# A row of reciprocal roots on GpSimd, and a scaling issued ahead of a one-column product

## The chip, the cores and the metric

The kernel runs on one core of a Trainium2 chip. A core has five engines with a queue of instructions each: TensorE (PE, matrix products into PSUM), VectorE (DVE), ScalarE (ACT), GpSimd (POOL) and SyncE (SP, which here only issues transfers). They meet through semaphores. The metric is the device time of one launch in microseconds.

## The reference

One encoder layer over 512 tokens of 1024 channels, and 256 memory tokens. What matters here is the branch of cross-attention into the memory, and the end:

```python
def rms_norm(x, g):
    xf = x.astype(F32)
    y = xf * lax.rsqrt(jnp.mean(xf * xf, axis=-1, keepdims=True) + EPS)
    return (y * g.astype(F32)).astype(x.dtype)
...
        y_ml = mlstm_branch(ml_q, ml_k, ml_v, ml_o, ml_gates, w_ml_conv[l], b_ml_conv[l],
                            b_ml_igate[l], b_ml_fgate[l], ml_norm_g[l])
...
        mem_k, mem_v = jnp.split(rms_norm(mem, mem_norm_g[l]) @ w_mem_kv[l], 2, axis=-1)
        y_xa = memory_cross_attention(xa_q, mem_k, mem_v)
...
        x = x + merged @ w_out[l]
        x = x + conv_glu_ffn(rms_norm(x, ffn_norm_g[l]), w_ffn_up[l], w_ffn_conv[l], b_ffn_conv[l], w_ffn_down[l])
    return rms_norm(x, final_norm_g)
```

The factor of `rms_norm` is one number a token. The kernel takes it out of the products and applies it to what they give.

## The kernel before, in words

Channels lie on the 128 partitions and tokens along the free axis until the last part. A weight block of 128 rows is loaded by SP (`emit_raw`), and split into a high part (`wh`, ScalarE, line 242) and the rest (`wl`, VectorE, line 243, from the two SBUF tiles `wr` and `wh`); each product is then three matmuls (`mm3`, lines 260 to 262). `weights(key)` keeps the split one block ahead of the matmuls: the split of block i+1 is issued when block i begins.

While the projections run, a generator for the bidirectional mLSTM (`ml_all`) is advanced by `step`. Each of its blocks `block(h, J)` makes a score tile on PE, a chain on VectorE (lines 800 to 814, among them line 805, a maximum over two small SBUF tiles, and line 810, which adds the two directions of the score tile `E`), then PE turns the tile (line 819) and multiplies it with the values (line 825). At a head's end a power of four columns runs on GpSimd (line 834).

The order on each engine is set when the kernel is built, from the program's order and the planner's own costs; `tc.issue_after(x)` ties instructions behind one that is given. At run time every engine takes its queue in order.

**The memory's norm.** During the projection "o" the squares of the memory are summed over channels by a matmul with ones (`square_sums`, line 355), so that every partition holds the row of sums of 256 tokens, in PSUM. Two things are made of it. `rstd_wide` (lines 369 to 377) makes the row of 1/rms on every partition: Ln and Exp(-0.5 x) on ScalarE, and three VectorE passes that improve the result by one Newton step. `rstd_cols` (lines 358 to 366) makes the same numbers as columns, one a partition: two VectorE reductions against the identity and a GpSimd power -0.5 of 128 x 2. The row `mrb` is first used at line 1165, where the first block of memory keys leaves PSUM; the columns `mrc` at line 1177, where the memory values do. Four PSUM banks (`mm`) hold the results of projections in turn.

**The end.** The last product is cut so that the last 128 tokens (row tile 3) end in two halves of their first 512 channels: one in `pa_[1]`, the other in `pl`. The second half's sum of squares is taken over 257 columns, the last being an extra column that carries the sum so far (line 1519, `rest`, written beside the matmuls' result in the bank `pl`). Row tile 2 (the second last 128 tokens) gets its factor `col2` by a GpSimd power (line 1360), its second half of channels is scaled on ScalarE (line 1518), its first half on VectorE (`scaled(2, 0, col2)`, line 1366), and one transfer stores it (line 1523). Row tile 3 ends with a power (line 1526), scalings (lines 1527 to 1530) and two transfers (lines 1528 and 1531).

Of the kernel before, what the change touches and what calls it, by code (L numbers as in the profile page):

```python
# [11 lines left out]
F32 = mybir.dt.float32  # L12
F32R = mybir.dt.float32r
AF = mybir.ActivationFunctionType
ALU = mybir.AluOpType
AX = mybir.AxisListType

P = 128
S = 512
D = 1024  # L20
KT = D // P
NT = S // P
M = 256
# [98 lines left out]
def hybrid_block(ctx, tc, xg, xT, memT, wflat, vecs, gbias, nabias, out):  # L122
    nc = tc.nc
    V, A, G, PE, SY = nc.vector, nc.scalar, nc.gpsimd, nc.tensor, nc.sync

    cp = ctx.enter_context(tc.tile_pool(name="cp", bufs=1))
# [10 lines left out]
    def nm(s):  # L137
        uid[0] += 1
        return f"{s}_{uid[0]}"

    def unit(dt=F32):
        return up.tile([P, UNIT], dt, tag="unit", name=nm("u"))

    def scr(n=512):
        return sp.tile([P, S], F32, tag="scr", name=nm("s"))[:, :n]

    def tiny(n):
        return tp.tile([P, 32], F32, tag="tiny", name=nm("y"), bufs=12)[:, :n]
# [174 lines left out]
    nhalf = cp.tile([P, 16], F32, name="nhalf")  # L323
    G.memset(nhalf, -0.5)
    msk = []
    for d in range(2):
        sgn = 1 if d == 0 else -1
        m = cp.tile([P, P], F32, name=f"msk{d}")
# [16 lines left out]
    def two_parts(acc, ntok):  # L345
        h, l = [sp.tile([P, S], F32R, tag="scr", name=nm("s"))[:, :ntok] for _ in range(2)]
        A.activation(h, acc, AF.Copy)
        V.tensor_tensor(l, acc, h.bitcast(F32), op=ALU.subtract)
        return h, l

    def square_sums(parts, ntok):

        ps = atps()
        for i in range(2):
            st["mm"] = PE.matmul(ps[:, :ntok], onesr, parts[i], start=i == 0, stop=i == 1).ins
        return ps

    def rstd_cols(ps, ntok, tag, n=D):

        nt = ntok // P  # L360
        v, junk = tiny(nt), scr(P)
        for t in range(nt):
            V.tensor_tensor_reduce(junk, ps[:, t * P:(t + 1) * P], ident, 1.0 / n, 0.0, ALU.mult, ALU.add,
                                   accum_out=v[:, t:t + 1])
        col = cp.tile([P, nt], F32, name=f"rc_{tag}")
        st["pool"] = G.tensor_tensor(col, v, nhalf[:, :nt], op=ALU.pow).ins
        return col

    def rstd_wide(ps, ntok, tag, n=D):

        v, y = scr(ntok), scr(ntok)
        rb = cp.tile([P, ntok], F32, name=f"rb_{tag}", tag=f"rb{ntok}", bufs=1)
        A.activation(v, ps[:, :ntok], AF.Ln, scale=1.0 / n)
        A.activation(y, v, AF.Exp, scale=-0.5)
        V.scalar_tensor_tensor(v, ps[:, :ntok], -0.5 / n, y, op0=ALU.mult, op1=ALU.mult)
        V.tensor_tensor(v, v, y, op=ALU.mult)
        V.scalar_tensor_tensor(rb, v, 1.5, y, op0=ALU.add, op1=ALU.mult)
        return rb
# [76 lines left out]
    def proj(key, XHs, XLs, n=S, at={}, ps=None):  # L455

        ws = weights(key)
        if (key[0], key[1]) in SUMS or key[0] in SUMS:
            sum_step(SUMS.get(key[0]) or SUMS[key[:2]], ws)
        k0 = 0 if ps is None else 1  # L460
        if ps is None:
            ps = mmps()
        for k in range(k0, KT):
            mm3(ps[:, :n], ws[k][0], ws[k][1], XHs[k], XLs[k], k == 0, k == KT - 1)
            if k == 1:
                flush()
            if k in at:
                at[k]()
        return ps
# [655 lines left out]
    def step(n=1):  # L1125
        quota[0] += n
        while quota[0] >= 1 and gens:
            try:
                next(gens[0])
                quota[0] -= 1  # L1130
            except StopIteration:
                gens.pop(0)
        if not gens:
            quota[0] = 0.0
# [11 lines left out]
    for f in range(4):  # L1146
        ps = proj(("o", f), XH, XL, at={3: lambda: step(RB / 2)})
        t = scr()
        V.tensor_tensor(t, ps, rb, op=ALU.mult)
        if f == 0:  # L1150
            so.append(unit())
        A.activation(so[0][:, f * S:(f + 1) * S], t, AF.Tanh, scale=0.5)
        if f == 0:
            msum = two_parts(macc, M)
        if f == 1:

            with tc.issue_after(st["mm"]):
                mps = square_sums(msum, M)
            mrb, mrc = rstd_wide(mps, M, "m"), rstd_cols(mps, M, "m")
        step(RB / 2)  # L1160
    mkv = unit()
    mk, mv = mkv[:, 0:1024], mkv[:, 1024:2048]
# [17 lines left out]
    for f in range(4):  # L1180
        ps = proj(("naq", f), XH, XL, at={3: lambda: step(RB / 2)})
        V.tensor_tensor(nq[:, f * S:(f + 1) * S].rearrange("p (b r c) -> p b r c", r=ROWS, b=4), rv(ps), rv(rb),
                        op=ALU.mult)
# [103 lines left out]
    def cv(t, f):  # L1287
        o = t % 2 * D + f * S
        return C[t // 2][:, o:o + S]
# [49 lines left out]
    ss = [sv[:, 2 * t:2 * t + 2] for t in range(NT)]  # L1339
# [16 lines left out]
    def power(t, v, f):  # L1356

        col = tiny(1)
        V.tensor_tensor(col, ss[t][:, f:f + 1], v, op=ALU.add)
        G.tensor_tensor(col, col, nhalf[:, :1], op=ALU.pow)  # L1360
        return col

    def scaled(t, f, col, dst=None):

        dst = cv(t, f) if dst is None else dst
        V.scalar_tensor_tensor(dst, cv(t, f), col, gfin[:, f * S:(f + 1) * S], op0=ALU.mult, op1=ALU.mult)
# [122 lines left out]
    vs = {}  # L1489
# [21 lines left out]
    col2 = power(2, vs[2], 0)  # L1511
    sqa = squares(pa_[1][:, one_], 3, 0)
    v = tiny(1)
    V.tensor_tensor(v, ss[3][:, 0:1], vs[3], op=ALU.add)
    col = tiny(1)
    G.tensor_tensor(col, v, nhalf[:, :1], op=ALU.pow)
    with tc.issue_after(sqa):
        A.activation(cv(2, 1), cv(2, 1), AF.Copy, scale=col2)
    rest = V.scalar_tensor_tensor(pl[:, Hf:Hf + 1], v, D ** 0.5, col, op0=ALU.mult, op1=ALU.mult).ins
    with tc.issue_after(rest):  # L1520
        V.tensor_tensor(oa[:, one_], pa_[1][:, one_], gfin[:, one_], op=ALU.mult)
        scaled(2, 0, col2)
    SY.dma_start(out[2 * P:3 * P, :], C[1][:, :D])
    v, sq, col = tiny(1), scr(), tiny(1)
    A.activation(sq[:, :Hf + 1], pl[:, :Hf + 1], AF.Square, scale=D ** -0.5, accum_out=v)
# [114 lines left out]
```

## Time and profile before

| | us |
|---|---|
| median of 3 runs | 858.49 (857.82 to 859.49) |
| profiled execution | 858.62 |
| its span | 856.9 |
| PE busy | 849.4 (99%) |
| VectorE busy | 644.7 (75%) |
| ScalarE busy | 482.0 (56%) |
| GpSimd busy | 164.2 (19%) |

A row of the timeline gives the start, the duration, the engine, the line of the kernel, the operation, the tile written and the tiles read, their shapes and a count; in brackets stands how long the engine was idle before it and what ended that. "PEclk" is the granted clock of TensorE, 1.00 at its full speed. In the view of windows the columns are the window, its length, then busy time and count for PE, the loads of PE, VectorE, ScalarE and GpSimd, then the clock, the busy share of the 16 DMA engines and GB/s.

### The profile page before, as it was taken

To read this page: it belongs to the slowest core of one execution; us is meant where nothing else is said; L and a number is where in the kernel's file an instruction comes from. 1 tells how busy PE (TensorE), PEld (TensorE's weight loads), DVE (VectorE), ACT (ScalarE), POOL (GpSimd) and SP (SyncE) were. 2 spreads that over 40 slices of the span, in tenths; PEclk is the share of its full clock that TensorE was granted. 3 is DMA by queue.
4 is the path that set the end of the run, shared out by engine and by line. 5 is a ranking of instruction groups with operands and counts; after the bars stand their busy time and mean duration, and the time that the engine had idled before them with its cause. 6 is when DMAs were issued, how large, how long until landed. Compare 5 with 4: busy or idle time off the path is not lost.

```text
span 856.9 us, 12273 instructions
## 1 busy us (share of the span) xinstructions
PE 849.4 (99%) x4116; PEld 716.2 (84%) x4116; DVE 644.7 (75%) x1372; ACT 482.0 (56%) x1025; POOL 164.2 (19%) x279
## 2 busy tenths in 40 slices
PE   9999999999999999999999999999999999999996
PEld 7898988988888888888888888888888888888885
DVE  7696597877568758898668657877786777788886
ACT  7354456666546648888644445444464444446763
POOL 0100100001113594601101002222100333320001
PEclk9999999999999999999999999999999999999999
DMA  8226764643675655549755954677265222326663
GB/s 280 93 75 162 241 187 123 184 116 109 232 195 132 205 149 145 163 146 236 276 160 145 264 157 135 161 157 250 85 187 181 76 97 99 99 74 216 190 205 139
DMA packets 77023, 139.80 MB, mean 163 GB/s; under 512 B 38232, under 2 KB 45400, under 8 KB 75360
## 3 DMA queue, kind: packets, MB, share of 16 engines
q1 hardware_dynamic: 67184, 109.24, 40.6%
q0 software_dynamic: 9344, 29.39, 14.5%
q8 instruction: 32, 0.52, 0.2%
q10 hardware_dynamic: 432, 0.39, 0.1%
q14 instruction: 31, 0.25, 0.1%
HBM read 130.84 MB, written 31.21 MB: 189 GB/s over the span
## 4 chain that ended last, share of the span: by engine, by line
PE 97%; DVE 1%; DMA 0%; ACT 0%; issue 0%; POOL 0%; POOLq 0%; DVEq 0%
PE mm L260 25%; PE mm L262 25%; PE mm L261 25%; PE at L1330 2%; PE at L1328 2%; PE at L1329 2%; PE at L261 2%; PE at L260 2%; PE at L262 2%; PE mm L1330 1%; PE mm L1328 1%; PE mm L1329 1%; PE at L999 1%; PE at L980 1%; PE at L768 1%; PE at L792 1%
## 5 line engine op out<-in xcount | busy, mean ns | idle before, releaser
L260 PE MATMUL mm<-u,wh 128*128 128x512 f32 (+1 forms) x907 | 353.9, 390 | 0.0
L262 PE MATMUL mm<-u,wl 128*128 128x512 f32 (+1 forms) x907 | 350.2, 386 | 0.0
L261 PE MATMUL mm<-u,wh 128*128 128x512 f32 (+1 forms) x907 | 350.0, 386 | 0.0
L242 ACT ACTIVATE wh<-wr 128x512 fp32r<-128x512 f32 (+2 forms) x328 | 203.2, 625 | 172.6 <-PE mm L261 111.6
L243 DVE TENSOR_TENSOR wl<-wr,wh 128x512 fp32r<-128x512 f32 (+2 forms) x330 | 236.2, 719 | 62.7 <-ACT wh L242 56.6
L262 PEld LDWEIGHTS mm<-u,wl 128*128 128x128 f32 x907 | 170.5, 188 | 34.6
L260 PEld LDWEIGHTS mm<-u,wh 128*128 128x128 f32 x907 | 170.8, 188 | 33.1 <-ACT u L266 0.3
L261 PEld LDWEIGHTS mm<-u,wh 128*128 128x128 f32 x907 | 170.7, 188 | 33.1 <-DVE u L267 0.2
L618 POOL DMA_DIRECT2D u<-nav_d x128 | 62.7, 533 | 27.1 <-PE at L999 16.7
L1432 POOL TENSOR_TENSOR s<-s,rb 128x512 f32<-128x512 f32 x18 | 29.4, 1634 | 155.9 <-DVE s L1431 148.6
L169 POOL COPY y<-wl 128x1 f32<-128x1 f32 x24 | 5.9, 246 | 178.7 <-DVE wl L243 177.6
L1328 PE MATMUL at<-wh,u 128*128 128x512 f32 x100 | 39.1, 391 | 0.0
L1330 PE MATMUL at<-wh,u 128*128 128x512 f32 x100 | 38.9, 389 | 0.0
L1329 PE MATMUL at<-wl,u 128*128 128x512 f32 x100 | 38.9, 389 | 0.0
L1377 ACT ACTIVATE u<-r 128x256 fp32r<-128x256 f32 x44 | 17.7, 414 | 36.3 <-DVE r L1446 23.1
L518 ACT ACTIVATE s<-pad,vec 128x512 f32<-128x512 f32 x30 | 24.3, 811 | 19.1 <-DVE pad L516 19.1
L519 DVE SCALAR_TENSOR_TENSOR s<-pad,vec,s 128x512 f32<-128x512 f32 x30 | 23.0, 765 | 5.0 <-ACT s L518 4.9
L1428 ACT ACTIVATE s<-s 128x512 f32<-128x512 f32 x22 | 13.9, 633 | 19.9 <-DVE s L520 19.8
L1378 DVE TENSOR_TENSOR u<-r,u 128x256 fp32r<-128x256 f32 x44 | 20.4, 474 | 5.7 <-ACT u L1377 5.7
L1431 DVE SCALAR_TENSOR_TENSOR s<-s,s 128x512 f32<-128x512 f32 x22 | 15.2, 691 | 11.9 <-ACT s L1430 11.9
L520 DVE SCALAR_TENSOR_TENSOR s<-pad,vec,s 128x512 f32<-128x512 f32 x30 | 22.5, 748 | 0.7
L1330 PEld LDWEIGHTS at<-wh,u 128*128 128x128 f32 x100 | 18.8, 188 | 3.9
(343 smaller groups left out, 1249.4 us busy)
## 6 DMA issues: line engine op xcount, KB each, us to landing
wr<-wflat SPq DMA_DIRECT2D x140, 512.0 KB, 3.7
wr<-wsum_T SPq DMA_DIRECT2D x20, 512.0 KB, 4.1
wsum_T<-wflat POOLq DMA_DIRECT2D x8, 1024.0 KB, 9.0
wsum_T<-wflat POOLq DMA_DIRECT2D x6, 768.0 KB, 7.3
nab<-nabias SPq DMA_DIRECT2D x16, 256.0 KB, 2.8
u<-nav_d POOLq DMA_DIRECT2D x128, 32.0 KB, 2.9
s<-xT SPq DMA_DIRECT2D x15, 256.0 KB, 4.7
nav_d<-nv POOLq DMA_DIRECT2D x8, 256.0 KB, 2.9
```

The costliest lines, as they stand in the source:

```text
L242: st["hi"] = A.activation(h[:, u:v], src, AF.Copy).ins
L243: st["lo"] = V.tensor_tensor(l[:, u:v], src, h[:, u:v].bitcast(F32), op=ALU.subtract).ins
L260: PE.matmul(ps, lh, rh, start=start, stop=False)
L261: PE.matmul(ps, lh, rl, start=False, stop=False)
L262: st["mm"] = PE.matmul(ps, ll, rh, start=False, stop=stop).ins
L518: A.activation(t1, pad[:, 0:512], AF.Identity, scale=vcol(w, i), bias=vcol(b, i))
L519: V.scalar_tensor_tensor(t1, pad[:, 1:513], vcol(w, n + i), t1, op0=ALU.mult, op1=ALU.add)
L618: G.dma_start(vw[r * 32:(r + 1) * 32, i * 256:(i + 1) * 256], nav_v[hf, r, CW[b]:CW[b] + 32, hp * 256:(hp + 1) * 256])
L1328: PE.matmul(bank, ah[:, ts], w[0], start=start, stop=False, skip_group_check=True)
L1329: PE.matmul(bank, ah[:, ts], w[1], start=False, stop=False, skip_group_check=True)
L1330: st["mm"] = PE.matmul(bank, al[:, ts], w[0], start=False, stop=True, skip_group_check=True).ins
L1432: ve.tensor_tensor(c, c, rb2, op=ALU.mult)
```

## The change

Two places change. The row of the memory's 1/rms is no longer made by `rstd_wide`: ScalarE copies the sums out of PSUM, scaled by 1/1024, into `mv2`, the columns are made as before, and GpSimd raises the 256 columns of `mv2` to the power -0.5 (the exponent is the first column of `nhalf`, repeated). At the end, the scaling of row tile 2's first half is tied behind the sum `vadd` and stands ahead of the extra column in the program, where it was tied behind that column.

```diff
-            mrb, mrc = rstd_wide(mps, M, "m"), rstd_cols(mps, M, "m")
+            mrb, mv2 = cp.tile([P, M], F32, name="rb_m"), scr(M)
+            A.activation(mv2, mps[:, :M], AF.Copy, scale=1.0 / D)
+            mrc = rstd_cols(mps, M, "m")
+            G.tensor_tensor(mrb, mv2, nhalf[:, :1].to_broadcast([P, M]), op=ALU.pow)
...
-    V.tensor_tensor(v, ss[3][:, 0:1], vs[3], op=ALU.add)
+    vadd = V.tensor_tensor(v, ss[3][:, 0:1], vs[3], op=ALU.add).ins
     col = tiny(1)
     G.tensor_tensor(col, v, nhalf[:, :1], op=ALU.pow)
     with tc.issue_after(sqa):
         A.activation(cv(2, 1), cv(2, 1), AF.Copy, scale=col2)
+    with tc.issue_after(vadd):
+        scaled(2, 0, col2)
     rest = V.scalar_tensor_tensor(pl[:, Hf:Hf + 1], v, D ** 0.5, col, op0=ALU.mult, op1=ALU.mult).ins
     with tc.issue_after(rest):
         V.tensor_tensor(oa[:, one_], pa_[1][:, one_], gfin[:, one_], op=ALU.mult)
-        scaled(2, 0, col2)
```

## The prediction

> **What bounds the kernel now.** I read the page's engine row and chain of waits first, then who TensorE waits for, then the two places of the change by the timeline.
>
> ```profile
> PE 849.4 (99%) x4116; PEld 716.2 (84%) x4116; DVE 644.7 (75%) x1372; ACT 482.0 (56%) x1025; POOL 164.2 (19%) x279
> PE 97%; DVE 1%; DMA 0%; ACT 0%; issue 0%; POOL 0%; POOLq 0%; DVEq 0%
> PE at L289 <- PEq L1633: 0.8, 1, 0.8
> ```
>
> The third line is the whole answer of the view of waits for PE: in the whole span it waits once, 0.8 us at the start. So TensorE's stream sets the end, and the matmuls leave only the last microseconds to others. Work taken off another engine in the middle is worth nothing; a new wait of PE costs its full length, since no idle time is left to give it back. The profiled execution took 858.62 us, its span 856.9, so 1.7 lie around it; the median is 858.49, 0.13 less. Sums below start from 858.6.
>
> **The memory's row: what goes.**
>
> ```profile
> 130.50 0.41 PE L355 MATMUL at<-s,onesr 128*128 128x256 f32 x2
> 131.17 1.28 ACT L373 ACT_TABLE_LOAD   x1
> 132.47 0.38 ACT L373 ACTIVATE s<-at 128x256 f32<-128x256 f32 x1
> 132.87 1.28 ACT L1152 ACT_TABLE_LOAD   x1
> 134.70 0.40 ACT L374 ACTIVATE s<-s 128x256 f32<-128x256 f32 x1
> 131.31 0.68 DVE L243 TENSOR_TENSOR wl<-wr,wh 128x512 fp32r<-128x512 f32 x1
> 135.13 0.42 DVE L375 SCALAR_TENSOR_TENSOR s<-at,s 128x256 f32<-128x256 f32 x1 [3.14 <-ACT s L374]
> 136.23 0.42 DVE L377 SCALAR_TENSOR_TENSOR rb_m<-s,s 128x256 f32<-128x256 f32 x1
> 136.23 0.08 DVE L363 DVE_READ_ACCUMULATOR2_ANT y<- 128x1 f32 x1
> 136.40 0.84 POOL L366 TENSOR_TENSOR rc_m<-y,nhalf 128x2 f32<-128x2 f32 x1 [22.24 <-DVE y L363]
> 147.58 0.42 DVE L1165 TENSOR_TENSOR u<-mm,rb_m 128x256 f32<-128x256 f32 x1
> ```
>
> Gone are Ln and Exp (0.38 + 0.40), the load of Ln's table and of the one that brings the others back (2 x 1.28), and three VectorE passes, of which the first and last are shown (3 x 0.42). A Copy of Ln's shape (0.38) comes in. ACT gains 2.96 us, VectorE 1.26 and a wait of 3.14: all of it beside matmuls that never waited, so **0 on the path**.
>
> **What comes: one power over 256 columns.** No row has this shape. Bounds come from the power on few columns and from GpSimd's ordinary product on this shape:
>
> ```profile
> 849.40 0.55 POOL L1516 TENSOR_TENSOR y<-y,nhalf 128x1 f32<-128x1 f32 x1
> 230.68 1.04 POOL L834 TENSOR_TENSOR y<-y,nhalf 128x4 f32<-128x4 f32 x1 [7.21 <-DVE y L832]
> 232.21 0.69 DVE L1210 TENSOR_TENSOR s<-mm,rb_x 128x512 f32<-128x512 f32 x1 [1.68 <-PE mm L262]
> 184.59 1.25 POOL L834 TENSOR_TENSOR y<-y,nhalf 128x4 f32<-128x4 f32 x1 [23.53 <-DVE y L832]
> L1453 POOL TENSOR_TENSOR r<-r,u 128x256 f32<-128x256 f32 x9 | 6.6, 738 | 7.2 <-DVE u L1446 7.2
> ```
>
> One column 0.55, four 1.04, the latter with VectorE idle beside it (its 1.68 before 232.21): (1.04 - 0.55) / 3 = 0.163 us a column. 256 columns: 0.55 + 255 x 0.163 = **42.1 us**. The product's rate (0.74) is the lower end; the slowest four columns give (1.25 - 0.55) / 3 = 0.233 and 60 us. From two columns (0.84) to four it is 0.10, so 0.84 + 254 x 0.10 = 26 us. I take 42: same operation, measured undisturbed; the product does not compute a power. The doubt is that a long run may go by a faster loop than four columns.
>
> The Trainium skill, "GPSIMD Engine Reference", section 3.1, puts a two-input pass at about 2.6 cycles an element and core, at 1.2 GHz: an estimate from it is 0.55 us and a start-up for 256 columns, and the sum would be that of the rival "short power" below. The four columns speak against applying it to a power.
>
> When it starts: the sums are ready at about 131 and VectorE is free at 132.0. Its two column reductions lie between L375 and the last reading at 136.23, with one pass of 0.42 among them, so some 0.85 us; the small power took 0.84. That makes about 133.7 in the program's order. The row is there at 133.7 + 42.1 = **175.8**, where 136.65 was. The 11 us left until L1165 at 147.58 are used up, and 28 more.
>
> **Who waits: the shared input.** Two pairs show what an operation on GpSimd does to one on VectorE that reads two SBUF tiles:
>
> ```profile
> 556.79 0.73 POOL L1449 TENSOR_TENSOR r<-r 128x256 f32<-128x256 f32 x1 [1.71 <-DVE u L1378]
> 556.81 1.27 DVE L243 TENSOR_TENSOR wl<-wr,wh 128x512 fp32r<-128x512 f32 x1
> 31.25 1.03 POOL L366 TENSOR_TENSOR rc_x<-y,nhalf 128x4 f32<-128x4 f32 x1 [28.71 <-DVE y L363]
> 31.61 0.69 DVE L243 TENSOR_TENSOR wl<-wr,wh 128x512 fp32r<-128x512 f32 x1 [0.46 <-ACT wh L242]
> ```
>
> L243 takes 0.69 alone; beside a product of 256 columns it takes 1.27 and ends 0.56 after it: it did nothing until GpSimd had finished. Beside a power of four columns it takes 0.69: once four columns are read, nothing is held. With 256 columns reading lasts as long as computing, unless GpSimd can buffer most of them. So I expect VectorE's operations with two SBUF inputs to stand still from 133.7 to about 175.8. The Trainium skill, "SBUF — State Buffer", section "Who interferes with whom", has it that such a pair excludes each other for the whole instruction, whoever starts first; the second pair shows less than that for a short power, the first pair agrees.
>
> What is behind it on VectorE and PE:
>
> ```profile
> 137.71 0.16 DVE L805 SCALAR_TENSOR_TENSOR y<-y,em 128x2 f32<-128x2 f32 x1
> 139.79 0.35 DVE L810 SCALAR_TENSOR_TENSOR E<-E,y 128x128 f32<-128x128 f32 x1
> 140.33 0.27 PE L819 MATMUL at<-ident,E 128*128 128x128 f32 x1
> 148.24 0.68 DVE L243 TENSOR_TENSOR wl<-wr,wh 128x512 fp32r<-128x512 f32 x1
> 151.75 0.28 PE L262 MATMUL mm<-u,wl 128*128 128x256 f32 x1
> 850.00:850.50 0.50, 0.16 (x2) 0.00 (x0) 0.23 (x2) 0.21 (x2) 0.00 (x0) 1.00 0.00 0
> 853.50:854.00 0.50, 0.00 (x0) 0.00 (x0) 0.00 (x0) 0.00 (x0) 0.00 (x0) 0.50 0.96 365
> ```
>
> L805 reads two small SBUF tiles and begins the chain to L810, whose block PE turns at 140.33; PE is in order, so everything behind that turn waits. That chain took 2.4 us with other work between (137.71 to 140.14), and its two shown ends alone make 0.5. By the first, PE resumes at 175.8 + 2.4 = 178.2: **37.9 us lost**, 36.0 by the second. PE's clock falls from 1.00 to 0.50 some 3 us after its last matmul (the window rows at 850 and 853.5; the clock is the column ahead of the DMA share). After such a stall it starts slow; no row shows the way back. If it takes 3 us too, half of them are lost: an estimate of +1.5, bounds 0 and 3.
>
> If the power runs long but VectorE isn't shut out, L1165 alone waits, and behind it VectorE's queue: the split at 148.24 for the third memory block, whose matmuls follow about 151.8. VectorE comes to that split's end 1.3 us after L1165's start (148.92 - 147.58), so at 177.1, and PE loses 25.3.
>
> On GpSimd's own queue the heads' powers come next (184.59 is the second's), themselves behind VectorE; its transfers for weight sums are issued from the projection "nak" on, later in the program. They move with the rest.
>
> **The tail.**
>
> ```profile
> 849.47 0.72 ACT L1518 ACTIVATE u<-u,y 128x512 f32<-128x512 f32 x1 [0.49 <-POOL y L1360]
> 850.27 0.17 DVE L1519 SCALAR_TENSOR_TENSOR at<-y,y 128x1 f32<-128x1 f32 x1 [1.11 <-PE at L1330]
> 850.68 0.74 DVE L1366 SCALAR_TENSOR_TENSOR u<-u,y,u 128x512 f32<-128x512 f32 x1
> 851.03 0.81 POOL L1526 TENSOR_TENSOR y<-y,nhalf 128x1 f32<-128x1 f32 x1 [1.07 <-ACT s L1525]
> 851.50 0.33 SPq L1523 DMA_DIRECT2D out<-u  x1
> 852.64 0.33 SPq L1531 DMA_DIRECT2D out<-s  x1
> 852.00:852.50 0.50, 0.00 (x0) 0.00 (x0) 0.50 (x2) 0.50 (x1) 0.00 (x0) 1.00 0.38 147
> 852.50:853.00 0.50, 0.00 (x0) 0.00 (x0) 0.11 (x1) 0.09 (x1) 0.00 (x0) 1.00 1.05 426
> 854.50:855.00 0.50, 0.00 (x0) 0.00 (x0) 0.00 (x0) 0.00 (x0) 0.00 (x0) 0.50 1.00 365
> ```
>
> The scaling (L1366, 0.74) moves into VectorE's wait of 1.11 ahead of the extra column (L1519): its factor is there at 849.47, as ACT's use shows, so it ends at 850.21, and L1519, which waits for PE's last matmul, starts at 850.27 as before. Beside the last power it is gone: 0.81 falls towards 0.55, -0.26 on the path. The third tokens' transfer leaves at about 850.3, not 851.5. Today it and the last two share full engines from 852.5 to 855.0 (five half-microsecond rows, first and last shown under the row before them); 0.8 us lie from issue to first bytes (851.5 to 852.3, as that row's share of 0.38 has it). Moved, the last 512 KB start at 852.38 + 0.8 and take 1.3 at 400 GB/s: 854.5, where 855.05 was. **-0.55**, bounds -1.2 (the whole advance) and +0.5 (the scaling shuts out the power of L1516 that starts 0.07 before it).
>
> Sum: 858.6 + 37.9 + 1.5 - 0.55 = **897.5**.
>
> **The rivals.**
> - *Long power, VectorE not shut out* (0.20). For it: the pair at 31.25. 858.6 + 25.3 + 1.5 - 0.55 = 884.9.
> - *Middling power, 26 us* (0.11), by the step from two columns to four; against it, the two were measured beside VectorE. All is 15.9 us sooner: 881.6 shut out, 869 not.
> - *Short power* (0.29), the other side: the loop over many columns runs at up to 16 ns a column, near the product's 0.74 us in all. The row must then be there before L805 runs at 137.7, so a power of at most 4.0 us, or 13.9 (147.58 - 133.7) without shutting out. PE never waits, only the tail counts: 858.6 - 0.55 = 858.05, no change. For it: the same engine does 256 ordinary products in 0.74; against it: 0.163 a column.
> - *Faster* (0.03): the short power with the tail's whole advance and a little of PE's order: 856.7.
>
> **How the numbers follow.** The forecast has 0.37, at 897.5, its own range 892 (small power second in GpSimd's queue, no slow clock, quickest chain) to 900 (slow clock at its 3 us and the tail's +0.5). A measurement of this kernel can tell about 0.2%, 1.7 us, from no change. Slower: 0.37 + 0.20 + 0.11 = 0.68, and 0.02 of the short power at 10 us, shut out: 0.70. Same 0.27, faster 0.03. Without the short power 3 in 10 are left out, so the range goes down to it: 857.0 to 900. The 60 us power (915) stays outside.
>
> **What would show it.** Right: a POOL power at L1162 of about 42 us from 133 on, L243 or L805 stretched over it, PE idle from 140 to 178, PEclk at 0.5 in that slice. VectorE waiting at L1165 for POOL, with L243 at 0.69 before: the second case. A power of a few microseconds and no wait of PE: the short one, and my rate per column was wrong. Tail: L1366 ahead of L1519, the last power at 0.55, the third transfer's issue near 850.3, each counted from PE's end.

## The result, and the profile after

| | before | after |
|---|---|---|
| median, us | 858.5 (857.82 to 859.54) | 891.7 (890.69 to 891.82) |
| ratio | | 1.0382 [1.0368, 1.0395] |
| span of the profiled execution, us | 856.9 | 890.0 |

The change costs 33.2 us. The engine row and the chain of waits of the page after:

```profile
PE 853.0 (96%) x4116; PEld 719.5 (81%) x4116; DVE 644.6 (72%) x1369; ACT 479.5 (54%) x1022; POOL 205.5 (23%) x280
PE 92%; POOL 5%; DVE 1%; ACT 1%; DMA 0%; issue 0%; POOLq 0%; DVEq 0%; ACTq 0%
```

The whole list of what PE waited for after (total, times, longest):

```profile
PE at L825 <- ACT E L820: 28.4, 1, 28.4
PE at L768 <- ACT H L812: 1.3, 1, 1.3
PE at L289 <- PEq L1637: 0.8, 1, 0.8
```

GpSimd has come into the chain with 5% of the span, and PE, which had one wait of 0.8 us, has one of 28.4. Where from, the timeline after shows on GpSimd, VectorE, ScalarE and PE:

```profile
131.51 41.51 POOL L1162 TENSOR_TENSOR rb_m<-s,nhalf 128x256 f32<-128x256 f32 x1 [17.35 <-ACT s L1160]
173.01 0.69 POOL L366 TENSOR_TENSOR rc_m<-y,nhalf 128x2 f32<-128x2 f32 x1
132.99 0.16 DVE L805 SCALAR_TENSOR_TENSOR y<-y,em 128x2 f32<-128x2 f32 x1
134.02 0.35 DVE L810 SCALAR_TENSOR_TENSOR E<-E,y 128x128 f32<-128x128 f32 x1 [0.28 <-ACT E L809]
134.88 0.69 DVE L243 TENSOR_TENSOR wl<-wr,wh 128x512 fp32r<-128x512 f32 x1
173.73 0.16 DVE L808 TENSOR_TENSOR y<-y,ex 128x2 f32<-128x2 f32 x1 [33.48 <-POOL rc_m L366]
179.15 0.42 DVE L1168 TENSOR_TENSOR u<-mm,rb_m 128x256 f32<-128x256 f32 x1
173.99 0.37 ACT L812 ACTIVATE H<-at,y 128x128 f32<-128x128 f32 x1 [33.30 <-DVE y L808]
175.58 0.26 ACT L820 ACTIVATE E<-at 128x128 f32<-128x128 f32 x1
147.17 0.28 PE L262 MATMUL mm<-u,wl 128*128 128x256 f32 x1
175.90 0.80 PE L825 MATMUL at<-u,E 128*128 128x128 f32 x2 [28.45 <-ACT E L820]
180.83 0.56 PE L260 MATMUL mm<-u,wh 128*128 128x256 f32 x1
188.11 0.39 PE L825 MATMUL at<-u,E 128*128 128x128 f32 x2
```

Three things are to be seen. The power takes 41.51 us. While it runs, VectorE's operations with two SBUF inputs keep their length of before (L243 0.69 us, L805 0.16, L810 0.35): VectorE is not shut out. And VectorE doesn't wait where the row is used (L1168, line 1165 of before), but well ahead of it in its queue, at line 808, a tiny product that reads nothing GpSimd writes. The row names `rc_m` as what it waited for: the small power, which the planner put *behind* the long one.

Line 808 writes a fresh tile of the ring of tiny tiles, which has 12 buffers. In the built order its tile is the twelfth taken after the one that holds the memory's two column sums, which `rc_m` reads. In the program as built the two tiles have the same address. So the reading is: a buffer that can't be written until `rc_m` has read it.

From line 808 the wait reaches PE by way of ScalarE. Line 812 there needs what line 808 gives and stood for 33.30 us; line 820, which copies the turned tile out of PSUM for PE's line 825, comes behind it in ScalarE's queue, so PE stands too.

The loss by PE's place, each row against its counterpart before (before, the block of memory keys that starts here at 180.83 started at 148.91):

```profile
147.29 0.39 PE L825 MATMUL at<-u,E 128*128 128x128 f32 x2
148.91 0.36 PE L260 MATMUL mm<-u,wh 128*128 128x256 f32 x1
154.75 0.39 PE L825 MATMUL at<-u,E 128*128 128x128 f32 x2
```

L825 is 28.6 us late (175.90 against 147.29), the next block 31.9, the L825 after two blocks 33.4. The end of the span is 33.1 late, so the tail gave 0.3 back. The clock is in the windows of after (the number ahead of the DMA share):

```profile
145.00:150.00 5.00, 2.45 (x21) 2.24 (x19) 0.00 (x0) 0.00 (x0) 5.00 (x1) 1.00 0.00 0
150.00:155.00 5.00, 0.00 (x0) 0.00 (x0) 0.00 (x0) 0.00 (x0) 5.00 (x1) 0.50 0.00 0
183.00:184.00 1.00, 1.00 (x7) 1.00 (x7) 0.00 (x0) 0.43 (x1) 0.00 (x0) 0.50 0.04 12
184.00:185.00 1.00, 1.00 (x10) 1.00 (x10) 0.69 (x1) 0.20 (x1) 0.00 (x0) 0.94 0.00 0
```

It fell to half after PE's stop and came back at about 184.1. The two blocks from 180.83 took 7.28 us in place of 5.84: 1.4 us of half clock.

The tail after:

```profile
883.12 0.75 DVE L1369 SCALAR_TENSOR_TENSOR u<-u,y,u 128x512 f32<-128x512 f32 x1 [0.30 <-POOL y L1363]
883.29 0.28 PE L1333 MATMUL at<-u,u 128*128 128x256 f32 x1
883.79 0.16 DVE L1524 SCALAR_TENSOR_TENSOR at<-y,y 128x1 f32<-128x1 f32 x1
883.95 0.33 SPq L1527 DMA_DIRECT2D out<-u  x1
884.54 0.55 POOL L1530 TENSOR_TENSOR y<-y,nhalf 128x1 f32<-128x1 f32 x1 [0.93 <-ACT s L1529]
885.90 0.33 SPq L1535 DMA_DIRECT2D out<-s  x1
```

Counted from the end of PE's last matmul (883.57; 850.16 before): the scaling runs under the last matmuls, the third store leaves after 0.38 us (1.34 before), the last power takes 0.55 (0.81). The extra column starts at 0.22 (0.11), because the scaling ends late. The last store leaves at 2.33 (2.48).

### The profile page after: what moved, and what is told of

It reads as the page before. It is cut to its first block, busy times and chain, and to the rows that moved or that the text cites. A ratio compares the mean times of both kernels' runs of the same rounds, so it can differ in the third digit from the quotient of the medians.

```text
span 890.0 us, 12274 instructions
## 1 busy us (share of the span) xinstructions
PE 853.0 (96%) x4116; PEld 719.5 (81%) x4116; DVE 644.6 (72%) x1369; ACT 479.5 (54%) x1022; POOL 205.5 (23%) x280
## 4 chain that ended last, share of the span: by engine, by line
PE 92%; POOL 5%; DVE 1%; ACT 1%; DMA 0%; issue 0%; POOLq 0%; DVEq 0%; ACTq 0%
PE mm L260 24%; PE mm L261 24%; PE mm L262 24%; POOL rb_m L1162 5%; PE at L1331 2%; PE at L1333 2%; PE at L1332 2%; PE at L261 2%; PE at L260 2%; PE at L262 2%; PE mm L1331 1%; PE mm L1333 1%; PE mm L1332 1%; PE at L999 1%; PE at L980 1%; PE at L768 1%
## 5 line engine op out<-in xcount | busy, mean ns | idle before, releaser
L243 DVE TENSOR_TENSOR wl<-wr,wh 128x512 fp32r<-128x512 f32 (+2 forms) x330 | 236.3, 719 | 63.7 <-ACT wh L242 57.9
L1162 POOL TENSOR_TENSOR rb_m<-s,nhalf 128x256 f32<-128x256 f32 x1 | 41.5, 41508 | 17.4 <-ACT s L1160 17.4
L825 PE MATMUL at<-u,E 128*128 128x128 f32 x32 | 6.5, 286 | 28.4 <-ACT E L820 28.4
L825 PEld LDWEIGHTS at<-u,E 128*128 128x128 f32 x32 | 6.0, 196 | 29.7 <-ACT E L820 28.7
L808 DVE TENSOR_TENSOR y<-y,ex 128x1 f32<-128x1 f32 (+1 forms) x16 | 2.5, 156 | 33.8 <-POOL rc_m L366 33.5
L519 DVE SCALAR_TENSOR_TENSOR s<-pad,vec,s 128x512 f32<-128x512 f32 x30 | 23.0, 765 | 5.0 <-ACT s L518 4.9
```

What stands on the lines that cost most here:

```text
L243: st["lo"] = V.tensor_tensor(l[:, u:v], src, h[:, u:v].bitcast(F32), op=ALU.subtract).ins
L1162: G.tensor_tensor(mrb, mv2, nhalf[:, :1].to_broadcast([P, M]), op=ALU.pow)
```

## The experiments

All kernels but one were timed against the kernel of before; medians and ratios with their intervals.

**The buffer.** e1 gives the two column sums a buffer of their own:

```diff
-        v, junk = tiny(nt), scr(P)
+        v = tiny(nt) if tag != "m" else cp.tile([P, nt], F32, name="v_m")
+        junk = scr(P)
```

> The changed kernel, with a buffer of its own for the two column sums that the small power rc_m reads (before: one of the 12 buffers of the ring of tiny tiles). Theory A: the long wait of VectorE at L808 is for that ring buffer, which rc_m, queued behind the 41.5 us power, releases late. Then L808 no longer waits; VectorE goes on to the first use of the row (near 147) and waits there until the row is ready at 173.0. PE then has the second memory block's weights too and stops at about 152 instead of 147.45, resuming near 174.3: a stall of 22.3 us, with 3.6 us of slow clock and -0.3 at the end 858.5 + 25.6 = 884. Theory B: VectorE is shut out of the second SBUF input while the power runs, or waits for the row itself: VectorE stops at 140.3 as before and the time stays at 891.7.

Measured: 880.9 us, ratio 1.026 [1.0245, 1.0275]. Its timeline (lines are one higher here, so line 808 is L809):

```profile
139.53 0.16 DVE L809 TENSOR_TENSOR y<-y,ex 128x2 f32<-128x2 f32 x1
172.29 0.42 DVE L1169 TENSOR_TENSOR u<-mm,rb_m 128x256 f32<-128x256 f32 x1 [25.43 <-POOL rb_m L1163]
173.57 0.58 PE L262 MATMUL mm<-u,wl 128*128 128x256 f32 x1 [20.52 <-DVE wl L243]
```

The wait at line 808 is gone and a new one of 25.4 us has come at the row's first use; PE stands 20.5 us in the third memory block, for its weights' low part. Theory A's mechanism holds, B falls. The time is 3 us below A's number: PE ran to 153.0, not 152, was let go at 173.6, not 174.3, and by the windows its clock was back 4.3 us after the first matmul, where the changed kernel took 8.2.

**The order on GpSimd.** e2 ties the long power behind the small one:

```diff
+            with tc.issue_after(st["pool"]):
-            G.tensor_tensor(mrb, mv2, nhalf[:, :1].to_broadcast([P, M]), op=ALU.pow)
+                G.tensor_tensor(mrb, mv2, nhalf[:, :1].to_broadcast([P, M]), op=ALU.pow)
```

> The changed kernel, with the power over the row tied behind the small power rc_m on GpSimd's queue. Theory A (ring buffer): rc_m ends near 133.4 and frees its buffer, L808 doesn't wait; the row is ready at about 174.9, 1.9 us later than with its own buffer, and its first use waits: stall 24.2 us, about 886. Theory B (shut out): VectorE stops at its first operation with two SBUF inputs near 133.4, and the time is 891 to 895.

Measured: 882.81 us, ratio 1.0283 [1.0266, 1.0301].

```profile
132.79 0.73 POOL L366 TENSOR_TENSOR rc_m<-y,nhalf 128x2 f32<-128x2 f32 x1 [18.62 <-DVE y L363]
133.51 41.12 POOL L1163 TENSOR_TENSOR rb_m<-s,nhalf 128x256 f32<-128x256 f32 x1
140.55 0.16 DVE L808 TENSOR_TENSOR y<-y,ex 128x2 f32<-128x2 f32 x1
174.66 0.42 DVE L1169 TENSOR_TENSOR u<-mm,rb_m 128x256 f32<-128x256 f32 x1 [27.02 <-POOL rb_m L1163]
```

The ring is untouched here, and line 808 runs at 140.55 without a wait: it was the small power's place in the queue that held its buffer. Again A holds and B falls; the time is 3 us below A's 886, since PE waited 22.1 us and not 24.2. This is also the order that the prediction assumed, so it shows what that order costs: 24.5 us over the 858.28 of before beside it, with one long wait of VectorE, at the row's first use.

**The length of the power.** e3 has `ALU.mult` in place of `ALU.pow`; e4 raises only the first 128 or 64 columns to the power and multiplies the rest:

```diff
-            G.tensor_tensor(mrb, mv2, nhalf[:, :1].to_broadcast([P, M]), op=ALU.pow)
+            G.tensor_tensor(mrb[:, :128], mv2[:, :128], nhalf[:, :1].to_broadcast([P, 128]), op=ALU.pow)
+            G.tensor_tensor(mrb[:, 128:], mv2[:, 128:], nhalf[:, :1].to_broadcast([P, M - 128]), op=ALU.mult)
```

> The changed kernel with a product in place of the power over the row, on the same tiles and in the same place of the queue; the row of 1/rms is therefore left out and the memory keys are scaled by another number. If the length of the power alone makes the loss: the instruction takes about 0.74 us, PE doesn't wait, and the time is that of before with the end's gain, 858.2. If something else of the first edit costs (the Copy, the reordered queues, the buffer ring), 1 to 33 us of the loss stay.

Measured: 858.25 us, ratio 0.9998 [0.9989, 1.0008]: same. PE has its one wait of before, and the instruction on GpSimd is short:

```profile
131.57 0.95 POOL L1162 TENSOR_TENSOR rb_m<-s,nhalf 128x256 f32<-128x256 f32 x1 [17.35 <-ACT s L1160]
```

> The changed kernel with the power over 128 of the 256 columns and a product over the other 128, so the row is 1/rms for half of the memory tokens only. At 0.162 us a column the power takes 20.8 us and the product about 0.5 to 0.7; rc_m then ends near 153.8 and VectorE resumes 19.9 us sooner than in the changed kernel. PE resumes near 156, a stall of 8.5 us from 147.45 and 1.3 after it, 3.6 more if the clock still falls: 858.5 + 13.1 = 871.6, or 868 with the clock kept. A power with a high start-up and a faster rate would give less than half of the loss.

Measured: 871.32 us, ratio 1.015 [1.0135, 1.0166], as expected, PE's waits too:

```profile
PE at L825 <- ACT E L820: 8.4, 1, 8.4
PE at L768 <- ACT H L812: 1.3, 1, 1.3
```

> The changed kernel with the power over 64 of the 256 columns and a product over the other 192, so the row is 1/rms for a quarter of the memory tokens only. The power takes 10.4 us, the product 0.6, rc_m ends near 143.3; VectorE waits 3 us at L808 (140.3), PE, which stops at 147.45, finds its tile by 145.5. No stall of PE: 858.2. By the prediction's lock, VectorE would stop from 131.5 to 142 and PE lose some 4 us: 862.

Measured: 859.15 us, ratio 1.001 [1.0001, 1.0019]. PE has one more wait than before, for ScalarE, which stood behind VectorE at line 808; that wait, less the tail's gain, is what is left:

```profile
PE at L768 <- ACT H L812: 0.9, 1, 0.9
```

The timeline rows of the powers, of 128 columns and then, in the other kernel, of 64 with VectorE's wait:

```profile
130.76 21.11 POOL L1162 TENSOR_TENSOR rb_m<-s,nhalf 128x128 f32<-128x128 f32 x1 [17.36 <-ACT s L1160]
```

```profile
131.17 10.91 POOL L1162 TENSOR_TENSOR rb_m<-s,nhalf 128x64 f32<-128x64 f32 x1 [17.35 <-ACT s L1160]
143.26 0.16 DVE L808 TENSOR_TENSOR y<-y,ex 128x2 f32<-128x2 f32 x1 [3.35 <-POOL rc_m L366]
```

10.91, 21.11 and 41.51 us for 64, 128 and 256 columns: 10.20 for 64 more, 20.40 for 128 more, 0.159 us a column. In the changed kernel's order the loss goes with that length; while the instruction is short (e3), the Copy, the freed tables and the new order cost nothing that shows. At full length the order does cost, through the buffer: e1 and e2, without that wait, are 9 to 11 us faster with the same power.

**The clock.** e6 fills PE's stall with 120 matmuls into a bank that nobody reads:

```diff
         ps = proj(("memk", f), MH, ML, M)
+        if f == 0:
+            warm = mmps()
+            with tc.issue_after(st["mm"]):
+                for _ in range(120):
+                    PE.matmul(warm, onesr, XH[0], start=True, stop=True)
```

> The changed kernel with 120 extra matmuls of 512 columns behind the first memory block, into a PSUM bank that nobody reads: they fill 27 of the 28.4 us of PE's stall. If the half clock after the stall costs 3.6 us (the loss of 33.2 less the waits of 28.4 and 1.3, and the end's gain), the time falls to about 888 and the clock stays at 1.00 after the stall. If those microseconds come from VectorE and ScalarE catching up, the time stays at 891.7 or rises by the fillers that outlast the stall.

Measured: 891.03 us, ratio 1.0378 [1.0364, 1.0392], which overlaps the changed kernel's. PE in the timeline:

```profile
146.55 28.16 PE L1172 MATMUL mm<-u,onesr 128*128 128x512 f32 x120
175.16 0.49 PE L825 MATMUL at<-u,E 128*128 128x128 f32 x2 [0.46 <-ACT E L820]
178.79 1.66 PE L768 MATMUL at<-u 128*128 128x129 f32 x6 [2.14 <-ACT H L812]
180.10 0.56 PE L260 MATMUL mm<-u,wh 128*128 128x256 f32 x1
```

The window with its clock:

```profile
175.00:180.00 5.00, 2.69 (x14) 2.31 (x15) 4.86 (x18) 3.47 (x11) 0.00 (x0) 0.87 0.52 157
```

Of the two expectations the second came: the time stays about where it was, and the clock did not stay up. The long power began at 130.77 in this execution, and the next memory block 49.3 us later; in the changed kernel it was 180.83 - 131.51 = 49.3 too. PE came to line 825 at full clock, and then waited 2.14 us for ScalarE in place of 1.3: catching up on VectorE and ScalarE sets that point, not the clock. The clock fell in that wait all the same (0.87 as the mean of the window). The two blocks from 180.10 took 6.71 us (L825 follows at 186.81), 0.9 more than before and 0.6 less than in the changed kernel, too little for the timing to tell. What the clock costs by itself is thus bounded by the 1.4 us of the changed kernel's two slow blocks; the runs don't measure it more closely.

**The shared input.** e8 has 40 products in a row in place of the power:

```diff
-            G.tensor_tensor(mrb, mv2, nhalf[:, :1].to_broadcast([P, M]), op=ALU.pow)
+            for _ in range(40):
+                G.tensor_tensor(mrb, mv2, nhalf[:, :1].to_broadcast([P, M]), op=ALU.mult)
```

> The changed kernel with 40 products over the 256 columns in a row in place of the one power, so the row of 1/rms is left out and the memory keys are scaled by another number. They take 30 us in all. A probe of the shared input: if any GpSimd instruction that reads SBUF shuts VectorE out, as a long power was expected to, the two are alike and L243 keeps its 0.69 us in both. If what counts is how densely GpSimd reads, L243 and the other operations with two SBUF inputs stretch here to 1.2 us or more, while they keep their length beside the power. The time itself follows rc_m's end near 162: about 880, more if VectorE gets nothing done beside the products.

Measured once: 870.67 us. GpSimd and VectorE in the timeline:

```profile
136.21 25.54 POOL L1163 TENSOR_TENSOR rb_m<-s,nhalf 128x256 f32<-128x256 f32 x35
136.21 0.63 DVE L805 SCALAR_TENSOR_TENSOR y<-y,em 128x2 f32<-128x2 f32 x1
137.70 0.65 DVE L810 SCALAR_TENSOR_TENSOR E<-E,y 128x128 f32<-128x128 f32 x1 [0.17 <-ACT E L809]
139.20 0.94 DVE L243 TENSOR_TENSOR wl<-wr,wh 128x512 fp32r<-128x512 f32 x1
```

Line 805 goes from 0.16 to 0.63 us, line 810 from 0.35 to 0.65, L243 from 0.69 to 0.94. So products do hold VectorE's operations with two SBUF inputs up and the power doesn't. They don't hold them until they are through, either: the 35 products follow each other at 0.73 us (25.54 / 35), and by these rows L243, 0.69 us alone, was still done in 0.94. That it is the density of GpSimd's reads fits both, and is not shown beyond that; L243 stretched less than expected. The time was a miss: the planner put `rc_m` behind the fifth product. VectorE waited 13.0 us at the row's first use instead, and PE 8.6 us for a weight split behind that.

**The tail.** e5 is the kernel of before with the second edit alone.

> The second edit alone: the kernel of before with the scaling of row tile 2's first half tied behind the sum, ahead of the extra column. Counted from PE's last matmul the changed kernel ended 0.3 us sooner than before, so 858.2: a ratio of 0.9997, which the rounds may not tell from 1. In the trace: the last power at 0.55 us instead of 0.81, the extra column 0.1 us later after PE's end, the third store's issue about 1 us sooner. The prediction's term was -0.55.

Measured: 858.33 us, ratio 0.9996 [0.9987, 1.0005]: same. Its end in the timeline:

```profile
849.54 0.75 DVE L1366 SCALAR_TENSOR_TENSOR u<-u,y,u 128x512 f32<-128x512 f32 x1 [0.30 <-POOL y L1360]
850.03 0.28 PE L1330 MATMUL at<-u,u 128*128 128x256 f32 x1
850.42 0.17 DVE L1521 SCALAR_TENSOR_TENSOR at<-y,y 128x1 f32<-128x1 f32 x1
850.36 0.33 SPq L1524 DMA_DIRECT2D out<-u  x1
851.18 0.55 POOL L1527 TENSOR_TENSOR y<-y,nhalf 128x1 f32<-128x1 f32 x1 [1.16 <-ACT s L1526]
```

Its span ends at 856.6, 6.29 us after PE's last matmul, where before took 6.74 and the changed kernel 6.43. The last power fell to 0.55 us as expected, and the third store left 1.3 us sooner; the extra column (L1521) was not late here: 0.11 us after PE's end, as before. It now stands behind the scaling, and so hangs on when the factor of row tile 2 comes: in e3 it starts 0.42 us after PE's end and in e8 0.79. The other traces with this edit took 6.20 to 6.61 us for the end, e8 6.96. So the edit gains up to half a microsecond and can lose 0.2, which is too small for the timing. No kernel here is measurably faster than before.

## Why the prediction was right, and where it was wrong

Direction and size came out: 897.5 was forecast, 891.7 measured, 0.3 below the forecast's own range of 892 to 900. But the mechanism that stood behind the number was the wrong one, and that the number came so close is in part luck.

- *PE bounds, and what is taken from ScalarE and VectorE is worth nothing*: right. e3 keeps these savings and stays at 0.9998.
- *42.1 us for the power, from one and four columns*: right, 41.51. This step carried the forecast. The other end, the rate of an ordinary product, is out. The Trainium skill, "GPSIMD Engine Reference", section 3.1, has about 2.6 cycles an element for a two-input pass, measured there on an add; for this power 0.159 us a column makes 191 cycles at that page's 1.2 GHz (an estimate), so the figure doesn't carry over.
- *Start at 133.7, small power first*: the long power began 2.2 us earlier, at 131.51, and the planner put it first. The prediction had this only as the lower end of its own range and asked what it saved, not what would then stand behind a 41.5 us instruction.
- *VectorE shut out of its second SBUF input*: wrong, the step that failed. L243 ran at its 0.69 us inside the power. The pair of rows that it rested on had an ordinary product; the pair at 31.25, which spoke against, was read as an effect of its four columns. Even the first pair says less than was read into it: L243 ended 0.56 us after the product, sooner than its 0.69 alone, and e8 shows it done in 0.94 among products without a pause. The Trainium skill, "SBUF — State Buffer", section "Who interferes with whom", has an exclusive lock between such a pair; the trace after shows none beside a power.
- *PE stops at 140.3 and loses 37.9*: it stopped at 147.45 and lost 28.4 and 1.3. The chain of lines 805 to 810 that was to block it ran inside the power, unhindered; what stopped VectorE was line 808 two blocks on.
- *A wait for a buffer*: in no rival. The rival "long power, VectorE not shut out", with the row's first use as the only wait, was put at 884.9. e2 is that case in the order assumed, at 882.8, and e1 at 880.9: its mechanism is real but lay hidden behind the earlier wait, and removing that wait gains 11 us only, because the next one stands 25 us long behind it.
- *+1.5 for the clock*: about right for the two slow blocks (1.4), but by chance: the way back took 8.2 us from PE's first matmul, where 3 was assumed. What PE lost at half clock before them was covered by the catching up: in e6, most of it at full clock, the way from L825 to the next block took 4.94 us, here 4.93.
- *-0.55 in the tail*: the sign right, 0.3 in the changed kernel's trace and 0.45 in e5's, within what single traces of this end differ by. The last power fell to 0.55 and the third store left 1.0 us sooner, as forecast; the extra column, costed at no delay, came 0.1 us late here and later in e3 and e8.

The stall was forecast 9.4 us too long (37.9 against 28.45): 7.1 because PE stopped later than forecast (147.45 against 140.33), 2.3 because it was let go sooner (175.90 against 178.2). Left out were 3.3 us of catching up behind it (L825 28.6 late, the next block 31.9). The two go against each other, and so, by luck, the sum came within 6 us. Not luck is that a power of some 42 us makes PE wait: it did so in the changed kernel, in e1 and in e2, by 20.5 us at the least. By what the runs show, the chance belonged on "long power, VectorE not shut out", with one wait more.

## What to carry to other kernels

Price an operation that the trace shows only on small shapes by the step between two of its own sizes, not by a cheaper operation on the right shape. When a long instruction goes into an in-order queue, list what the planner may put behind it, and for each of those who waits for its result and who waits for the buffers it reads: a ring of 12 tiny tiles stopped VectorE some 7 us of work ahead of the row's first use (139.5 against 146.9 in e1's timeline, where it was not stopped). Where a wait is removed, look for the next one behind it before counting the gain.

## What the runs showed of the hardware

- GpSimd's power -0.5 on 128 partitions goes at 0.159 us a column from 64 to 256 columns, with 0.7 us beside it; the same instruction as a product took 0.95 us for all 256 in e3.
- Beside that power VectorE's operations with two SBUF inputs keep their length; beside back-to-back products the three shown stretch by 0.25 to 0.47 us (e8).
- By windows of half a microsecond PE's clock fell to half 2.5 us after the last matmul in the changed kernel, 4.3 us after it in e1 and 2.0 us after it in e6, where PE stood for 2.14 us only: no fixed delay. It was back at 184.1 in the changed kernel, 8.2 us after the first matmul at 175.90, with a wait of 1.3 us between; in e1, without a wait, 4.3 us after it.
- The mean clock of such a window tells where in it the change lies (0.98 from 149.5 to 150.0 puts the fall at 149.98). From the fall to the return went 34.13 us in the changed kernel, 23.90 in e2, 20.48 in e1, 13.65 in e4 with 128 columns, 10.24 in e8 and 3.41 in e6: 10, 7, 6, 4, 3 and 1 times 3.41. So in these six traces the clock changed only in steps of that length. That the place of PE's stop and start within a step decides how long it runs slow fits them; no run tests it.
